# Folded input weights for a Fourier mixer, made in the FFN before it and kept in device memory

## The chip, the cores and the metric

One core of one Trainium2 chip. The time is the device time of one execution of the whole kernel in microseconds (us), as the median of several runs; less is better. The engines are TensorE (PE, matrix products, with its weight loads as PEld), VectorE (DVE), ScalarE (ACT), GpSimd (POOL) and SyncE (SP), whose queue issues nearly all transfers (DMA).

## The reference

One inference step of a small transformer-like trunk: 512 latent and 128 context tokens of width 1024, two layers. A layer is a half-step FFN, a token mixer, and another half-step FFN. Each sub-layer is wrapped in two RMS norms and is shifted, scaled and gated by vectors ("modulation") that come from a conditioning vector. Layer 0 mixes by a Fourier transform, layer 1 by attention.

```python
def _modulation(cond, w_mod, b_mod):
    m = jax.nn.silu(cond) @ w_mod + b_mod
    return m.reshape(cond.shape[0], N_MOD, D_MODEL)

def _half_ffn(x, m, k, g_pre, g_post, w1, w2):
    h = _modulated_prenorm(x, g_pre, m, k)
    return x + 0.5 * m[:, 3 * k + 2, None] * _rmsnorm(_swiglu(h, w1, w2), g_post)

def _fourier_mix(h, w_in, w_out):
    b, s, _ = h.shape
    u = (h @ w_in).reshape(b, s, N_FOURIER_GROUPS, FOURIER_GROUP_DIM)
    f = jnp.fft.fft2(u.astype(jnp.float32), axes=(1, 3), norm="ortho").real
    return f.astype(h.dtype).reshape(b, s, D_MODEL) @ w_out
```

The Fourier transform runs over the positions of a sequence and over the 128 channels of each of 8 groups. Context and latent tokens are separate sequences.

## The kernel before, in words

Six sub-layers follow one another: n = 0 is the first FFN (to about 440 us), n = 1 the Fourier mixer (to about 595), n = 2 and 3 are FFNs, n = 4 the attention, n = 5 the last FFN. Tokens lie in five tiles of 128: tiles 0 and 1, 3 and 4 are latent, 2 is the context tile.

**Products and splits.** Every fp32 operand is split into a high and a low half of a faster matmul type, and a product is three matmuls: high by high, low by high, high by low (`mm3`, lines 274 to 276). A split is a copy on ACT that gives the high half (line 260) and a subtraction on DVE that gives the low half (line 261). Weights come as *units* of 128 x 1024 numbers (512 KB). `unit(i)` makes sure that units up to i + 3 are sent: `send` loads one into a tile of the pool `raw` (4 buffers, through SP), prepares it by its kind, and splits it. The kind "fold" takes sum and difference of two halves of the weight on DVE before the split (lines 237 and 238); "block" splits into a ring of larger buffers; "plain" only splits.

**FFN.** The first layer runs in 22 blocks f of hidden channels (`w1_fast`), each with a fast scheme of seven products in place of eight. For it DVE adds gate and up weights (lines 228 to 230, tile `sums`, and 243), and these are split as well. A block first multiplies the gate's halves ("score" banks x, then y with the sums), then "turn" and "sum" banks follow. The second layer (`w2`) runs in five slices, after blocks 4, 8, 12, 16 and 22 (`SLICES`), tile by tile. While a slice of the second layer runs, the next block's gate and up units wait in two of the four raw buffers.

**Background work.** The modulation vectors of later sub-layers are matrix-vector products that PE doesn't do: `gemv` loads 512 KB of `w_mod_t` and multiplies and sums it twice on DVE (line 478, tile `junk`). These jobs are in a list, and `behind(n)` takes the next n of them. In FFN n, `BEHIND[n]` jobs are spread over the second layer's first four slices: 36 in the first FFN, 9 a slice. Others are taken at fixed places of the mixer.

**The end of the first FFN.** A finished tile goes through `chain` (its boundary): ACT squares it and sums (line 626), DVE multiplies by the gate vector (627, 630), POOL takes the power for the norm (610), DVE adds to the residual (633), and later it is transposed by PE, scaled and split into the mixer's input. The next tile's banks are first filled with partial sums by ACT (`seed`, line 913), and this waits until the tile that held the bank has gone through line 633.

**The mixer** (`fourier`). `pair_in` and the lines between multiply tokens with the eight four_in units into banks for even and odd channels; `sums` and `diffs` transform over positions, `channels` over channels; `pair_out` and what follows multiply with the eight four_out units. PSUM has 4 banks "main", 2 "score", 1 "turn" and 1 "sum"; a bank is free again when the split of its content is done.

**Order.** A scheduler orders each engine's instructions by estimated times and by priority; `high()` puts work ahead. An engine runs its own list in order, and waits at an instruction whose operands aren't there, with all behind it.

## Time and profile before

| | |
|---|---|
| median of 3 runs | 2216.58 us (2215.81 to 2218.85) |
| the profiled execution | 2218.44 us, its span 2216.7 us |
| mean clock granted to PE | 0.988 |
| busy: PE, DVE, ACT | 2173.2, 1743.1, 1179.2 us |
| transfers | 293.25 MB |

A line of the profile gives the line of the code, the engine, what is written from what, how many (x) and how long, and often the idle time just before and what ended it (`<-`). In the windows each engine's busy time in a stretch stands before its count, and the clock is a share of full speed.

### The profile page before, as it was taken

The numbers are of one execution on the slowest core, as the hardware profiler recorded it, in microseconds if no ns is written. First come the engines' busy times: TensorE is split into PE (matmuls) and PEld (weight loads), VectorE is DVE, ScalarE is ACT, GpSimd is POOL, SyncE is SP. The second block draws the span as 40 slices with busy tenths as digits, with TensorE's granted clock in tenths as the row PEclk, the third lists the DMA queues.
The fourth block names the chain that finished last, engine by engine and source line by source line (L and its number), as shares of the span: only waits on it lengthen the run. The fifth ranks groups of instructions, "written<-read, shape, count | busy, mean of one in ns | idle before, by whom it ended". The sixth has DMA issues, their size and how long they took to land.

```text
span 2216.7 us, 34573 instructions
## 1 busy us (share of the span) xinstructions
PE 2173.2 (98%) x13299; PEld 1997.3 (90%) x13299; DVE 1743.1 (79%) x3218; ACT 1179.2 (53%) x2221; POOL 45.3 (2%) x95
## 2 busy tenths in 40 slices
PE   7999999999899999999999999999999999999998
PEld 5999999977699999898998999989998899999997
DVE  5988898889798889878998898686556686766684
ACT  4544545464654545446544454466778654455452
POOL 0000000010100000001000000010000000000000
PEclk9999999998999999999999999999999999999999
DMA  8244344625324434452344444533333323322242
GB/s 315 86 143 162 134 152 139 216 86 178 116 96 138 159 132 147 148 196 99 109 147 146 141 143 146 179 99 101 111 101 110 119 81 105 115 95 77 95 129 100
DMA packets 85861, 293.25 MB, mean 132 GB/s; under 512 B 9696, under 2 KB 14656, under 8 KB 85568
## 3 DMA queue, kind: packets, MB, share of 16 engines
q1 hardware_dynamic: 85152, 290.39, 39.1%
q8 instruction: 104, 1.70, 0.3%
q10 hardware_dynamic: 544, 0.66, 0.1%
q14 instruction: 61, 0.50, 0.1%
HBM read 275.49 MB, written 11.58 MB: 130 GB/s over the span
## 4 chain that ended last, share of the span: by engine, by line
PE 89%; DVE 5%; ACT 3%; DMA 2%; issue 1%; POOL 0%; SPq 0%; DVEq 0%; POOLq 0%; ACTq 0%
PE main L275 12%; PE main L276 12%; PE main L274 12%; PE score L275 7%; PE score L276 7%; PE score L274 7%; PE turn L275 4%; PE turn L274 4%; PE sum L274 4%; PE sum L275 4%; PE turn L276 4%; PE sum L276 4%; DVE junk L478 1%; DMA raw<-in_w_mod_t 1%; PE sum L1569 1%
## 5 line engine op out<-in xcount | busy, mean ns | idle before, releaser
L260 ACT ACTIVATE hi<-raw 128x1024 fp32r<-128x1024 f32 (+1 forms) x388 | 371.1, 969 | 287.3 <-PE score L275 93.1
L261 DVE TENSOR_TENSOR lo<-raw,hi 128x1024 fp32r<-128x1024 f32 (+1 forms) x388 | 429.7, 1112 | 99.1 <-ACT hi L260 97.7
L274 PE MATMUL main<-hi,ring 128*128 128x512 f32 (+4 forms) x1089 | 412.3, 380 | 5.9 <-ACT hi L260 2.3
L275 PE MATMUL main<-lo,ring 128*128 128x512 f32 (+4 forms) x1089 | 410.8, 378 | 4.8 <-DVE lo L261 4.8
L276 PE MATMUL main<-hi,ring 128*128 128x512 f32 (+5 forms) x1089 | 410.3, 377 | 0.0
L478 DVE SCALAR_TENSOR_TENSOR junk<-raw,wide 128x1024 bf16<-128x1024 f32 x256 | 313.1, 1223 | 79.6 <-DMA raw<-in_w_mod_t 75.5
L276 PE MATMUL score<-ring,lo 128*128 128x320 f32 x916 | 283.4, 309 | 0.6 <-DVE lo L261 0.6
L275 PE MATMUL score<-ring,hi 128*128 128x320 f32 x916 | 283.7, 310 | 0.0
L274 PE MATMUL score<-ring,hi 128*128 128x320 f32 x916 | 283.3, 309 | 0.0
L274 PEld LDWEIGHTS main<-hi,ring 128*128 128x128 f32 (+2 forms) x1089 | 204.9, 189 | 47.9 <-ACT hi L260 3.6
L275 PEld LDWEIGHTS main<-lo,ring 128*128 128x128 f32 (+2 forms) x1089 | 205.9, 189 | 43.9 <-DVE lo L261 6.3
L276 PEld LDWEIGHTS main<-hi,ring 128*128 128x128 f32 (+2 forms) x1089 | 206.0, 189 | 40.5 <-issue 1.2
L274 PE MATMUL turn<-ring,hi 128*128 128x320 f32 x672 | 207.6, 309 | 3.0 <-ACT ring L260 2.9
L275 PE MATMUL turn<-ring,hi 128*128 128x320 f32 x672 | 208.3, 310 | 0.0
L274 PE MATMUL sum<-ring,hi 128*128 128x320 f32 x672 | 208.0, 310 | 0.1
L275 PE MATMUL sum<-ring,hi 128*128 128x320 f32 x672 | 207.8, 309 | 0.0
L276 PE MATMUL sum<-ring,lo 128*128 128x320 f32 x672 | 207.5, 309 | 0.0
L276 PE MATMUL turn<-ring,lo 128*128 128x320 f32 x672 | 207.0, 308 | 0.0
L942 ACT ACTIVATE y<-main 128x512 f32<-128x512 f32 x160 | 94.2, 591 | 208.2 <-PE main L276 207.0
L274 PEld LDWEIGHTS score<-ring,hi 128*128 128x128 f32 x916 | 172.4, 188 | 1.1
L276 PEld LDWEIGHTS score<-ring,lo 128*128 128x128 f32 x916 | 172.2, 188 | 1.0 <-DVE lo L261 1.0
L275 PEld LDWEIGHTS score<-ring,hi 128*128 128x128 f32 x916 | 172.3, 188 | 0.7
(318 smaller groups left out, 4138.8 us busy)
## 6 DMA issues: line engine op xcount, KB each, us to landing
raw<-in_w SPq DMA_DIRECT2D x272, 512.0 KB, 3.7
raw<-in_w_mod_t SPq DMA_DIRECT2D x128, 512.0 KB, 3.5
raw<-in_qkv SPq DMA_DIRECT2D x26, 512.0 KB, 3.5
spill<-ring SPq DMA_DIRECT2D x12, 640.0 KB, 3.3
ring<-spill SPq DMA_DIRECT2D x12, 640.0 KB, 7.4
raw<-in_bias SPq DMA_DIRECT2D x16, 448.0 KB, 3.7
first<-in_w_mod_k SPq DMA_DIRECT2D x8, 512.0 KB, 8.2
ring<-in_w_mod_k SPq DMA_DIRECT2D x8, 512.0 KB, 10.2
```

The costliest lines, as they stand in the source:

```text
L260: a = self.nc.scalar.activation(hi, src, AF.Copy)
L261: self.last_split = a, self.nc.vector.tensor_tensor(lo, src, hi.bitcast(F32), op=ALU.subtract)
L274: mm(out, whi, xhi, start=start, stop=False)
L275: mm(out, whi, xlo, start=False, stop=False)
L276: self.latest = mm(out, wlo, xhi, start=False, stop=stop)
L478: last = self.nc.vector.scalar_tensor_tensor(out=self.junk, in0=raw, scalar=1.0, in1=self.wide[:, cond, :], op0=ALU.mult, op1=ALU.mult, ac ...
L942: nc.scalar.activation(place(i, a), ps[a], AF.Copy)
L1569: mm = nc.tensor.matmul(out, cache_v[:, ds] if k is None else v[c // 2][c % 2][:, slot, ds], probs, start=n == 0, stop=n == len(tiles) - 1)
```

## The change

Eight jobs `fold_in` join the background list. Each loads one four_in unit, folds it on DVE, and stores it to device memory; the mixer then loads the folded units as plain ones. `BEHIND[0]` goes from 36 to 44, so that each of four slices takes two folds and nine modulation sums. Three modulation sums that the mixer's middle took are taken by blocks 19 to 21. Four splits of the mixer's middle are put at high priority. The odd bank of the first pair comes from "score" in place of "main". The second pair's output first asks for the units up to at + 7, that is all of four_out. The context tile is kept reversed in its 64 positions, so that 8 splits of a column fall away; constant tables follow.

```diff
-BEHIND = (36, 0, 36, 36, 0, 8)
+BEHIND = (44, 0, 36, 36, 0, 8)
...
+    def fold(self, a, b):
+
+        self.nc.vector.tensor_tensor(b, a, b, op=ALU.subtract)
+        self.nc.vector.scalar_tensor_tensor(out=a, in0=a, scalar=2.0, in1=b, op0=ALU.mult, op1=ALU.subtract)
+
+    def fold_in(self, k):
+
+        raw = self.raw_tile(self.io["four_in"][k])
+        a, b = (t.rearrange("p (m c) -> p m c", m=4) for t in (raw[:, :512], raw[:, 520:]))
+        self.fold(a[:, :, 2:], b)
+        self.nc.sync.dma_start(out=self.folded[k], in_=raw)
...
-                y = self.staged[:, 2 * j : 2 * j + n_pieces][:, :: -1 if j == CTX_TILE else 1]
+                y = self.staged[:, 2 * j : 2 * j + n_pieces]
+                if j == CTX_TILE:
+                    y = y[:, ::-1, :, ::-1]
...
-                if i in (1, 2):
-                    v, t, col = (2, SPECIAL, TOK + 1) if i == 1 else (5, 0, TOK)
+                if i == 1:
                     for c in range(0, NCH, 2):
-                        hi, lo = (h.block(part, c, 0)[:, :, col] for part in range(2))
-                        self.split(hi, lo, self.staged[:, v, c : c + 2, t])
+                        hi, lo = (h.block(part, c, 0)[:, :, TOK] for part in range(2))
+                        self.split(hi, lo, self.staged[:, 2, c : c + 2, SPECIAL])
...
                 w1_fast(a, half)
+                if n == 0 and a >= NF - 3:
+                    self.behind()
...
-                    self.units += [("foldblock" if k >= NWU else "fold", io["four_in"][k]) for k in range(NCH)]
+                    self.folded = [self.dram.tile([P, UNIT], F32, tag=f"fold{k}", name=self.name("fold")) for k in range(NCH)]
+                    self.units += [("block" if k >= NWU else "plain", self.folded[k]) for k in range(NCH)]
...
-            es, o = [self.bank() for _ in range(2)], self.bank()
+            es, o = [self.bank() for _ in range(2)], self.bank("main" if p else "score")
...
             p = [self.temp("left", F32R)[:, :322] for _ in range(2)]
-            self.split(*p, ps)
+            with high():
+                self.split(*p, ps)
...
-            self.split(*even_at(m, 0, 322), ps)
+            with high():
+                self.split(*even_at(m, 0, 322), ps)
...
-            self.behind((2, 2, 1, 0)[m])
+            self.behind(m < 2)
             self.unit(at + 3 + m)
...
+        self.unit(at + 4)
         pair_out(1)
...
+        for k in range(NCH):
+            self.background.insert(4 + 11 * k // 2, partial(self.fold_in, k))
```

What it does to the order shows at three places. First DVE's list at the end of the second slice (about 213 to 219 us of the profile before). `junk` is a modulation sum, `left` and `right` are the running block's intermediate products, `lo` of a `raw` is the next gate's low half, and `sums` the first of the three operations that add gate and up. Before:

```order
L478 SCALAR_TENSOR_TENSOR junk,mod<-raw_1969,wide 128x1024
L871 TENSOR_TENSOR left_1995<-score_852,left_1992 128x320
L478 SCALAR_TENSOR_TENSOR junk,mod<-raw_1969,wide 128x1024
L875 TENSOR_TENSOR left_2027<-left_1995,turn_1974 128x320
L261 TENSOR_TENSOR lo_1999<-raw_1996,hi_1998 128x1024
L879 TENSOR_TENSOR left_2027<-left_2027,sum_2030 128x320
L228 TENSOR_TENSOR sums_2033<-raw_1996,raw_2031 128x512
```

And in the changed kernel, where `raw_1992` is the slice's second fold:

```order
L888 TENSOR_TENSOR left_2055<-left_2055,sum_2058 128x320
L251 TENSOR_TENSOR raw_1992<-raw_1992 128x504
L486 SCALAR_TENSOR_TENSOR junk,mod<-raw_1997,wide 128x1024
L252 SCALAR_TENSOR_TENSOR raw_1992<-raw_1992 128x4x126
L486 SCALAR_TENSOR_TENSOR junk,mod<-raw_1997,wide 128x1024
L895 TENSOR_TENSOR right_2056<-left_2023,turn_2002 128x320
L269 TENSOR_TENSOR lo_2027<-raw_2024,hi_2026 128x1024
L900 SCALAR_TENSOR_TENSOR left_2023<-sum_2058,left_2023 128x320
L896 TENSOR_TENSOR right_2056<-right_2056,right_2021 128x320
L228 TENSOR_TENSOR sums_2061<-raw_2024,raw_2059 128x512
```

The fold's two operations stand around the last sum, and the gate's low half and the sums stand behind three more of the running block's products. SP's list of the same slice has the transfers, here in the changed kernel (before, it held the nine loads of `w_mod_t` and then the two of the next block, `in_w`):

```order
L203 DMA raw_1883<-in_w_mod_t 128x1024
L203 DMA raw_1915<-in_four_in 128x1024
L203 DMA raw_1920<-in_w_mod_t 128x1024
L259 DMA fold_80<-raw_1915 128x1024
L203 DMA raw_1952<-in_w_mod_t 128x1024
L203 DMA raw_1956<-in_w_mod_t 128x1024
L203 DMA raw_1988<-in_w_mod_t 128x1024
L203 DMA raw_1992<-in_four_in 128x1024
L203 DMA raw_1997<-in_w_mod_t 128x1024
L203 DMA raw_2024<-in_w 128x1024
L203 DMA raw_2059<-in_w 128x1024
L259 DMA fold_81<-raw_1992 128x1024
```

Two loads and two stores are added, and the load after the first store takes the buffer that this store reads. Second, DVE in the last slice of the first FFN (about 447 to 451 us before): `main_1047` and `main_1048` are the two halves of tile 1, `main_1049` the first half of the context tile, `col` the norm's column. Before:

```order
L609 SCALAR_TENSOR_TENSOR col_4279<-col_4275 128x1
L630 TENSOR_TENSOR main_1048<-main_1048,total_3829 128x512
L633 SCALAR_TENSOR_TENSOR ring_4102<-main_1047,col_4279,ring_4102 128x512
L633 SCALAR_TENSOR_TENSOR ring_4102<-main_1048,col_4279,ring_4102 128x512
L627 TENSOR_TENSOR main_1049<-main_1049,square_3832 128x512
```

In the changed kernel tile 1 is `main_1055` and `main_1056`, the context tile `main_1057`:

```order
L635 TENSOR_TENSOR main_1057<-main_1057,square_3884 128x512
L617 SCALAR_TENSOR_TENSOR col_4322<-col_4316 128x1
L617 SCALAR_TENSOR_TENSOR col_4333<-col_4329 128x1
L638 TENSOR_TENSOR main_1056<-main_1056,total_3881 128x512
L641 SCALAR_TENSOR_TENSOR ring_4162<-main_1055,col_4333,ring_4162 128x512
L641 SCALAR_TENSOR_TENSOR ring_4162<-main_1056,col_4333,ring_4162 128x512
```

The context tile's gate product has moved from behind tile 1's four operations to ahead of them. Third, DVE in the mixer's middle (about 519 to 524 us before): `rms` is the split of the small middle sums, `left` and `total` are the splits of sums and differences over positions, `raw` with line 237 or 251 a fold of four_out. Before:

```order
L237 TENSOR_TENSOR raw_4920<-raw_4920 128x512
L1142 TENSOR_TENSOR ring_4930<-raw_4928,ring_4930 8x1024
L238 SCALAR_TENSOR_TENSOR raw_4920<-raw_4920 128x512
L261 TENSOR_TENSOR rms_4934<-main_4935,rms_4933 8x322
L261 TENSOR_TENSOR left_4966<-main_4955,left_4965 128x322
```

And in the changed kernel:

```order
L269 TENSOR_TENSOR left_5002<-main_4991,left_5001 128x322
L269 TENSOR_TENSOR total_5014<-main_5005,square_5013 126x384
L269 TENSOR_TENSOR left_5028<-main_5017,left_5027 128x322
L251 TENSOR_TENSOR raw_4956<-raw_4956 128x512
L1154 TENSOR_TENSOR ring_4966<-raw_4964,ring_4966 8x1024
L269 TENSOR_TENSOR total_5040<-main_5031,square_5039 126x384
L252 SCALAR_TENSOR_TENSOR raw_4956<-raw_4956 128x512
L269 TENSOR_TENSOR rms_4970<-main_4971,rms_4969 8x322
```

Three of the splits now stand ahead of the third fold, and the middle's split has gone behind it.

More of the change, by code (lines that the diff above doesn't have):

```diff
@@ L233, in send @@
             raw = self.raw_tile(src)
-            a, b = raw[:, one], raw[:, two]
-            if "rows" not in kind:
-                a, b = a.rearrange("p (m c) -> p m c", m=4)[:, :, 2:], raw[:, 520:].rearrange("p (m c) -> p m c", m=4)
-            nc.vector.tensor_tensor(b, a, b, op=ALU.subtract)
-            nc.vector.scalar_tensor_tensor(out=a, in0=a, scalar=2.0, in1=b, op0=ALU.mult, op1=ALU.subtract)
+            self.fold(raw[:, one], raw[:, two])
         elif kind == "up":
@@ L245, in send @@
         n = at.stop - at.start
-        if kind in ("block", "foldblock", "foldrowsblock"):
+        if kind in ("block", "foldblock"):
             hi, lo = (self.ring(F32R)[:, :n] for _ in range(2))
@@ L1053, in list_units @@
                 if i == 0:
-                    self.units += [("foldblock" if k >= NWU else "fold", io["four_in"][k]) for k in range(NCH)]
+                    self.folded = [self.dram.tile([P, UNIT], F32, tag=f"fold{k}", name=self.name("fold")) for k in range(NCH)]
+                    self.units += [("block" if k >= NWU else "plain", self.folded[k]) for k in range(NCH)]
                     self.units += [("plain", io["dft"][k]) for k in range(3)]
-                    self.units += [("foldrowsblock" if u in (3, 4) else "foldrows", io["four_out"][u]) for u in range(NCH)]
+                    self.units += [("foldblock" if u in (3, 4) else "fold", io["four_out"][u]) for u in range(NCH)]
                 else:
@@ L1126, in fourier @@
         for k in range(NCH):
-            even_in(k, token(k, LAT + 64, TOK + 2), even)
+            even_in(k, token(k, LAT + 63, TOK + 1), even)
         plain, ends = self.ring(F32)[:64, :504], self.ring(F32R)
@@ L1175, in positions @@
             p = [self.temp("left", F32R)[:, :322] for _ in range(2)]
-            self.split(*p, ps)
+            with high():
+                self.split(*p, ps)
             ps = diffs(m)
             q = [self.temp(kind, F32R)[:126, :384] for kind in ("square", "total")]
-            self.split(*q, ps)
+            with high():
+                self.split(*q, ps)
             return p, q
@@ L1188, in channels @@
                 mm(x5, mid_w[0][:, 256 + 72 * m : 328 + 72 * m], p[i], start=m == i == 0, stop=False)
-            self.split(*even_at(m, 0, 322), ps)
+            with high():
+                self.split(*even_at(m, 0, 322), ps)
             ps = self.bank("score")[:, :384]
             self.mm3(ps, mid_w[0][:126, P : 2 * P], mid_w[1][:126, P : 2 * P], *q, True, True)
-            self.split(*odd_at(m, 0, 384), ps)
+            with high():
+                self.split(*odd_at(m, 0, 384), ps)
         ready = positions(0)
@@ L1707, in host_inputs @@
     ctx = np.arange(64)
+    back = ctx[::-1]
     big = np.zeros((3, P, UNIT))
@@ L1711, in host_inputs @@
     big[0, :, :516] = sums.reshape(2, P, 258).transpose(1, 0, 2).reshape(P, 516)
-    big[0, :65, 516:581] = wave(np.cos, np.arange(65), np.arange(65), CTX) / 128
+    big[0, :65, 516:581] = wave(np.cos, np.r_[64, back], np.arange(65), CTX) / 128
     big[0, 65, 581:838] = wave(np.cos, [256], np.r_[256, near], LAT) / 512
@@ L1726, in host_inputs @@
     small = np.zeros((P, 208))
-    small[:64, :64] = -wave(np.sin, ctx, ctx, CTX) / 128
+    small[:64, :64] = -wave(np.sin, back, ctx, CTX) / 128
     small[:64, 64:128] = -small[:64, :64]
```

## The prediction

> **What bounds the kernel now.** I read the page first: the span and the share of TensorE.
>
> ```profile
> span 2216.7 us, 34573 instructions
> ...
> PE 2173.2 (98%) x13299; PEld 1997.3 (90%) x13299; DVE 1743.1 (79%) x3218; ACT 1179.2 (53%) x2221; POOL 45.3 (2%) x95
> ```
>
> TensorE (PE) is idle for 2216.7 − 2173.2 = 43.5 us in all. So only three things count: whether an edit ends a wait of PE, starts one, or changes the clock that PE is granted. Next, busy time by stretches of the span: the end of a second-layer slice of the first FFN (200 to 240), the last blocks of that FFN (400 to 436), and the middle of the Fourier mixer (520 to 560). Columns are PE, PE's weight loads, DVE, ACT and POOL, then the granted clock, the DMA share and GB/s.
>
> ```profile
> 200.00:220.00 20.00, 20.00 (x114) 18.20 (x114) 18.60 (x33) 8.69 (x14) 0.00 (x0) 1.00 0.57 184
> 220.00:240.00 20.00, 20.00 (x139) 20.00 (x138) 19.80 (x34) 10.59 (x18) 0.00 (x0) 1.00 0.32 106
> 400.00:436.00 36.00, 36.00 (x221) 33.85 (x220) 29.53 (x49) 14.79 (x24) 0.00 (x0) 1.00 0.73 257
> 520.00:540.00 20.00, 16.37 (x78) 13.18 (x76) 19.21 (x33) 7.27 (x13) 0.00 (x0) 0.83 0.59 197
> 540.00:560.00 20.00, 17.65 (x51) 12.48 (x49) 16.59 (x32) 7.07 (x13) 0.00 (x0) 0.66 0.57 185
> ```
>
> In the FFN PE never stops and DVE runs just below it (38.40 of 40 us from 200 to 240). In the mixer DVE is as full, PE waits, and the clock drops. The timeline of PE there has these waits (start, length, instruction, and in brackets the idle time before it and what ended it):
>
> ```profile
> 451.00 0.50 PE L274 MATMUL main<-hi,ring 128*128 128x512 f32 x1 [0.56 <-ACT main L913]
> 473.91 0.49 PE L274 MATMUL main<-hi,ring 128*128 128x504 f32 x1 [1.24 <-DVE ring L633]
> 483.05 0.58 PE L275 MATMUL main<-lo,ring 128*128 128x256 f32 x1 [3.37 <-DVE lo L261]
> 522.10 0.39 PE L274 MATMUL main<-hi,ring 128*126 128x256 f32 x1 [1.77 <-DVE rms L261]
> 539.49 0.41 PE L274 MATMUL score<-left,hi 128*128 128x322 f32 x1 [1.85 <-DVE ring L261]
> 560.00 0.73 PE L274 MATMUL main<-hi,ring 128*128 128x512 f32 x2 [2.35 <-ACT hi L260]
> ```
>
> And the windows cut at the edges of the slow clock:
>
> ```profile
> 475.00:482.00 7.00, 4.68 (x25) 3.19 (x23) 6.56 (x16) 3.13 (x11) 0.59 (x1) 1.00 0.25 75
> 482.30:489.10 6.80, 6.05 (x19) 4.38 (x20) 6.80 (x10) 2.21 (x3) 0.00 (x0) 0.50 0.36 109
> 523.30:530.10 6.80, 6.80 (x26) 5.75 (x24) 6.80 (x13) 0.93 (x2) 0.00 (x0) 0.50 0.55 180
> 540.30:554.00 13.70, 13.70 (x35) 9.66 (x36) 12.10 (x26) 4.18 (x7) 0.00 (x0) 0.50 0.58 180
> 560.80:564.10 3.30, 2.84 (x7) 2.08 (x8) 0.41 (x1) 0.30 (x1) 0.00 (x0) 0.51 0.46 159
> ```
>
> The waits of 3.37, 1.77, 1.85 and 2.35 us are each followed by a stretch at clock 0.50; the one of 1.24 is not (clock 1.00 from 475 to 482). A usual stretch is 6.8 us long and costs half of that, 3.4 us. So a wait of about 1.8 us or more costs its own length and, most times, 3.4 us again.
>
> **The change, part by part.** Prices first, by shape, then transfers (KB, us from issue to landing):
>
> ```profile
> L478 DVE SCALAR_TENSOR_TENSOR junk<-raw,wide 128x1024 bf16<-128x1024 f32 x256 | 313.1, 1223 | 79.6 <-DMA raw<-in_w_mod_t 75.5
> L260 ACT ACTIVATE hi<-sums 128x1024 fp32r<-128x1024 f32 x79 | 83.9, 1062 | 121.3 <-DVE sums L230 109.4 <-PE sum L275 9.8 <-DVE right L887 1.1
> L237 DVE TENSOR_TENSOR raw<-raw 128x504 f32<-128x504 f32 x8 | 5.3, 680 | 2.1 <-DMA raw<-in_four_in 2.1
> L238 DVE SCALAR_TENSOR_TENSOR raw<-raw 128x504 f32<-128x504 f32 x8 | 5.3, 680 | 0.1
> ```
>
> ```profile
> raw<-in_w_mod_t SPq DMA_DIRECT2D x128, 512.0 KB, 3.5
> spill<-ring SPq DMA_DIRECT2D x12, 640.0 KB, 3.3
> raw<-in_four_in SPq DMA_DIRECT2D x8, 512.0 KB, 3.8
> x_out<-ring SPq DMA_DIRECT2D x8, 256.0 KB, 2.1
> ```
>
> **Folds in the FFN's slices.** Two fold jobs join the nine modulation sums of each of four slices. A fold is 0.68 + 0.68 = 1.36 us of DVE; with its load and store it holds a raw buffer for 3.8 + 1.4 + 3.3 = 8.5 us, where a sum holds one for 3.5 + 2 × 1.22 = 5.9. The store of 512 KB is in no row: it lies between those of 256 KB (2.1) and 640 KB (3.3), and I take 3.3, the nearer in size. This is DVE at the end of the slice that closes at 221 us, then PE there:
>
> ```profile
> 194.95 1.23 DVE L478 SCALAR_TENSOR_TENSOR junk<-raw,wide 128x1024 bf16<-128x1024 f32 x1
> 197.18 1.23 DVE L478 SCALAR_TENSOR_TENSOR junk<-raw,wide 128x1024 bf16<-128x1024 f32 x1 [0.99 <-DMA raw<-in_w_mod_t]
> 203.37 1.23 DVE L478 SCALAR_TENSOR_TENSOR junk<-raw,wide 128x1024 bf16<-128x1024 f32 x1 [1.12 <-DMA raw<-in_w_mod_t]
> 215.79 1.22 DVE L261 TENSOR_TENSOR lo<-raw,hi 128x1024 fp32r<-128x1024 f32 x1
> 218.77 0.69 DVE L230 TENSOR_TENSOR sums<-raw,raw 128x512 f32<-128x512 f32 x1
> 220.59 1.23 DVE L261 TENSOR_TENSOR lo<-sums,hi 128x1024 fp32r<-128x1024 f32 x1
> ```
>
> ```profile
> 221.47 0.31 PE L274 MATMUL score<-ring,hi 128*128 128x320 f32 x1
> 223.37 0.31 PE L275 MATMUL score<-ring,hi 128*128 128x320 f32 x1
> ```
>
> Only two of the four raw buffers turn over there; gate and up of the running block hold the others. So sums wait on loads (0.99, 1.12). The third sum ends at 194.95 + 1.23 = 196.2. In its buffer the first fold's weights land at 200.0, are folded by 201.4, and are stored by 204.7; only then can the sixth sum's load go out, and it lands at 208.2 instead of 203.3. From the sixth sum on DVE has no rest. Before, it took 215.79 − 203.37 = 12.4 us from there to the low half of the next gate. Now 1.9 us of splits fall into the pause ahead of it, and the second fold (1.36) and a small operation of 0.4 come in: about 12.3 us, so the low half starts near 220.5 instead of 215.8. The three operations for the sums of gate and up end, before, at 218.77 + 0.69 = 219.5, that is 3.7 us after that point. Now about 1.6 us of short products stand between as well: 220.5 + 3.7 + 1.6 = 225.8, and up to 1 us later where the low half itself lies in the queue longer. ACT's high half takes 1.06 more: 227.
>
> PE comes at 221.47. Its pace is (223.37 − 221.47)/13 = 0.146 us a matmul. Before, 12 matmuls use the gate and then the sums are wanted at 223.2. In the new order both halves of the gate come first, 24 matmuls, until 225.0. Six more need the high halves alone. So PE waits from 225.0 to between 227 and 228, and some tenths more for low halves: I take 2.6 us a slice, with ends of 0 (the store lands in 2.1, and the pauses swallow the fold) and 3.8. Four slices: 10.4 us, ends 0 and 15. A wait of that size gets the half clock in about 7 of 10 cases (four of four rows from 1.77 up, but here PE may wait in two pieces): 4 × 0.7 × 3.4 = 9.5. Sum **+19.9**, ends 0 and 29.
>
> The Trainium skill (TensorE: Matmul & The Clock Gate, Part 1 and "HAM oscillation") states that the clock halves after an idle window of some 3.4 us that runs freely, and that gaps over that length are to be avoided. By that rule these gaps of 2.6 us would cost 10.4 and not 19.9. The trace differs: half clock followed 1.77 us.
>
> **Three sums behind blocks 19 to 21.** 3 × 2 × 1.22 = 7.3 us more for DVE in some 36 us, where it has 36.00 − 29.53 = 6.5 to spare. PE was never stopped there, so the operands are ready ahead of it, and that lead hides the 0.8 left over: 0, with ends of 0 and +2 (a lead that is gone; nothing here can gain, since PE is full).
>
> **The last slice's context tile.** DVE and ACT before, as the third token tile's start is prepared:
>
> ```profile
> 447.45 0.22 DVE L609 SCALAR_TENSOR_TENSOR col<-col 128x1 f32<-128x1 f32 x2
> 448.78 1.41 DVE L633 SCALAR_TENSOR_TENSOR ring<-main,col,ring 128x512 f32<-128x512 f32 x2 [0.49 <-POOL col L610]
> 450.49 0.70 DVE L627 TENSOR_TENSOR main<-main,square 128x512 f32<-128x512 f32 x1 [0.30 <-ACT y L626]
> ```
>
> ```profile
> 449.77 0.60 ACT L626 ACTIVATE y<-main 128x512 f32<-128x512 f32 x1 [0.59 <-PE main L276]
> 450.35 0.59 ACT L913 ACTIVATE main<-y 128x512 f32<-128x512 f32 x1
> ```
>
> PE's next tile waits for ACT to fill the bank (L913), that for L633, that for POOL's power of the column. In the new order the context tile's gate product stands ahead of tile 1's column and L633. It can't start before 450.49, since ACT's square waits for PE. After it 0.7 + 0.2 + the way over POOL (447.67 to 448.78, 1.1): L633 at 452.4 instead of 448.78, its first half done at 453.1, the bank filled at 453.75. PE starts at 453.8 instead of 451.00: **+2.8**, ends 0 and 4, and 3.4 for the clock in 3 of 4 cases, **+2.6**.
>
> **The mixer.** Taking the odd bank of the first pair from the other pool ends the wait of 1.24: **−1.2**; after it nothing shorter waits. The wait of 3.37 stays: DVE between 462 and 483 does the boundary's chain, which the change leaves as it is but for 0.4 us of tiny splits; the 10.9 us of folds that leave the mixer (16 × 0.68) lay before and behind it, under a busy PE. The three waits after 520 (1.77 + 1.85 + 2.35 = 6.0) all end with a split that stood behind folds and sums on DVE, or with weights folded too late. There DVE is busy 19.21 of 20 us. Three sums fewer (7.3 us), splits at the front, and all output weights requested before the second pair: I take 0.85 × 6.0 = **−5.1**. The clock lost in their stretches is (6.8 + 13.7 + 3.3)/2 = 11.9; three quarters of it, **−8.9**. Ends: 0, and all of it, −17.9.
>
> Sum: 19.9 + 2.8 + 2.6 − 1.2 − 5.1 − 8.9 = +10.1. On the profiled execution's own 2218.4 (span 2216.7 and 1.7 around it) that is 2228.5. That execution lies 1.9 above the median of 2216.6, so on the median's footing the forecast is **2226.6**. By the page's rule for the four slices alone, the sum would be 0.6.
>
> **The rivals.**
>
> *The slices take the folds for nothing* (26%). For it: DVE has pauses of 0.99 and 1.12 us and more in front, and PE's order was moved to ask for the sums 1.8 us later. Against it: from the sixth sum on there is no pause left. It decides at 225.0: if the high half of the sums is there, no slice waits. Then 2216.6 + 2.8 − 1.2 − 17.9 + 1 (a rest at the slices) = 2201.3, faster.
>
> *Only a window idle as a whole halves the clock* (17%). A PE that is back after 2.6 us keeps full speed, and so does the one at 453.8. The mixer's gain stays, since its stretches are there: 10.4 + 2.8 − 1.2 − 5.1 − 8.9 = −2.0, giving 2214.6, the same as before. Against it: 1.77 us was enough at 522. The Trainium skill's rule (TensorE: Matmul & The Clock Gate, Part 1) is this rival's.
>
> *The mixer's waits don't yield* (15%). The chain from the product through ACT and DVE to the next bank is what is late, not the queue, and four_out's loads are late as well. Then the gain is −1.2 − 2 and the sum 19.9 + 5.4 − 3.2 = 22.1: 2238.7.
>
> **How the numbers follow.** The forecast has 42%, and its own range is 2217 to 2236 (two thirds of the slices' ends either way). Faster and slower both have weight, so the range reaches to the first rival's centre and the last one's: 2201 to 2239, which leaves out half of each, 13 + 7%. A measurement here can tell about 0.2%, 4.4 us. Faster by more: 24 of the first rival, 4 of the second: 0.28. Within: 2 of the first, 9 of the second, 6 of the forecast: 0.17. Slower: 36 of the forecast, 4 of the second, 15 of the last: 0.55.
>
> **What would show it.** In the changed profile: PE waits near 145, 225, 300 and 378 us, each released by ACT's or DVE's halves of the sums, with the clock at 0.50 behind; a wait of some 3 us before the tile that starts at 451; none at 474, 522 and 539. If those windows show PE 20.00 of 20.00, the first term fails and the kernel is faster. If the waits are there at clock 1.00, the second rival is right.

## The result, and the profile after

| | before | after |
|---|---|---|
| median of 4 runs each | 2217.02 us (2215.81 to 2218.85) | 2243.11 us (2240.06 to 2248.72) |
| ratio after : before, 95% interval | | 1.012 (1.0095 to 1.0144) |
| the profiled execution, its span | 2218.44, 2216.7 | 2240.06, 2238.3 |
| mean clock granted to PE | 0.988 | 0.985 |

The changed kernel is slower by 26 us, where 10 were forecast: the sign was right, the size was not, and the time lies above the range. The profiled execution is the fastest of its four (the others reach 2248.72 at a clock of 0.982), so the trace accounts for 21.6 us. The head of its page:

```profile
span 2238.3 us, 34596 instructions
...
PE 2179.4 (97%) x13299; PEld 2000.4 (89%) x13299; DVE 1742.4 (78%) x3214; ACT 1175.8 (53%) x2217; POOL 44.5 (2%) x95
```

DVE and ACT have four instructions fewer each: four splits of a column have fallen away, not eight. PE has 58.9 us of idle time instead of 43.5. To see where, I cut the span at three marks that both kernels have. The first is PE's product of `coef` with the identity near the end of the first FFN (400.31 before, 427.80 after). The second is the start of the tile behind the context tile (451.00, 483.01). The third is the first product behind the mixer (596.15, 618.48). Busy times by these stretches (columns as in the prediction), before:

```profile
220.00:300.00 80.00, 80.00 (x478) 74.64 (x477) 71.00 (x118) 41.30 (x64) 0.00 (x0) 1.00 0.42 139
...
400.30:451.00 50.70, 50.13 (x281) 44.91 (x278) 41.90 (x75) 21.27 (x46) 1.61 (x3) 1.00 0.61 216
451.00:596.10 145.10, 130.04 (x625) 101.00 (x625) 123.00 (x217) 85.35 (x174) 9.23 (x14) 0.89 0.35 116
596.10:2216.00 1619.90, 1608.20 (x10040) 1496.54 (x10040) 1240.73 (x2364) 875.24 (x1694) 32.02 (x70) 1.00 0.38 124
```

and after:

```profile
140.00:220.00 80.00, 77.91 (x447) 71.71 (x446) 66.02 (x108) 37.81 (x60) 0.00 (x0) 0.98 0.45 152
220.00:300.00 80.00, 75.27 (x415) 68.70 (x414) 66.44 (x109) 35.00 (x55) 0.00 (x0) 0.94 0.43 145
300.00:380.00 80.00, 76.80 (x452) 70.58 (x451) 67.19 (x112) 37.62 (x60) 0.00 (x0) 1.00 0.46 158
380.00:427.80 47.80, 43.58 (x263) 41.75 (x262) 42.63 (x75) 17.55 (x29) 0.00 (x0) 0.89 0.44 143
427.80:483.00 55.20, 50.32 (x280) 44.85 (x277) 46.92 (x84) 23.39 (x51) 1.61 (x3) 1.00 0.66 231
483.00:618.40 135.40, 123.79 (x625) 97.27 (x625) 109.71 (x190) 83.19 (x166) 8.32 (x14) 0.93 0.36 117
618.40:2238.00 1619.60, 1607.56 (x10040) 1495.83 (x10040) 1240.63 (x2364) 875.28 (x1694) 32.11 (x70) 1.00 0.38 124
```

By the marks, the FFN up to the first lost 427.80 − 400.31 = 27.5 us, the stretch to the next tile 55.2 − 50.7 = 4.5, the mixer gained 145.2 − 135.5 = 9.7, and the rest gained 0.7: 21.6. In the four FFN rows PE is idle for 2.1 + 4.7 + 3.2 + 4.2 = 14.2 us. The clock takes 80 × 0.02 + 80 × 0.06 + 47.8 × 0.11 = 11.7 more. Before, neither was there.

PE's timeline of the changed kernel has these waits:

```profile
147.18 0.41 PE L282 MATMUL score<-ring,hi 128*128 128x320 f32 x1 [0.53 <-ACT left L876]
...
150.69 0.42 PE L282 MATMUL score<-ring,hi 128*128 128x320 f32 x1 [1.47 <-ACT hi L268]
...
229.82 0.41 PE L284 MATMUL score<-ring,lo 128*128 128x320 f32 x1 [2.56 <-DVE lo L269]
...
232.45 0.63 PE L282 MATMUL score<-ring,hi 128*128 128x320 f32 x1 [0.53 <-ACT left L876]
...
237.49 0.64 PE L282 MATMUL score<-ring,hi 128*128 128x320 f32 x1 [1.47 <-ACT hi L268]
...
314.46 0.42 PE L284 MATMUL score<-ring,lo 128*128 128x320 f32 x1 [1.11 <-DVE lo L269]
...
397.28 0.41 PE L284 MATMUL score<-ring,lo 128*128 128x320 f32 x1 [2.15 <-DVE lo L269]
...
441.55 0.28 PE L595 MATMUL turn<-ident,coef 128*16 128x128 f32 x1 [1.17 <-DVE right L895]
...
483.01 0.50 PE L282 MATMUL main<-hi,ring 128*128 128x512 f32 x1 [3.72 <-ACT main L922]
...
515.89 0.39 PE L283 MATMUL main<-lo,ring 128*128 128x256 f32 x1 [3.17 <-DVE lo L269]
...
561.43 0.50 PE L282 MATMUL main<-hi,ring 128*128 128x512 f32 x1 [3.89 <-ACT ring L268]
```

Three of the four slices have three waits, not one: for the gate's low half, then 0.53 and 1.47. The first slice has only the pair. The pair comes with the same lengths in all four: PE puts both halves of the gate's products into the same bank, one after the other, so it waits 0.53 until ACT has copied the first (L876), and then 1.47 for the sums' high half. The windows around some of them:

```profile
146.40:160.00 13.60, 11.51 (x64) 10.71 (x63) 11.22 (x18) 5.36 (x9) 0.00 (x0) 0.87 0.36 114
229.00:240.00 11.00, 8.18 (x31) 7.38 (x32) 7.89 (x13) 5.46 (x9) 0.00 (x0) 0.59 0.20 61
310.00:325.00 15.00, 11.80 (x75) 10.74 (x75) 13.61 (x22) 6.85 (x11) 0.00 (x0) 1.00 0.46 146
560.00:580.00 20.00, 18.34 (x56) 13.29 (x57) 14.07 (x26) 8.42 (x15) 0.00 (x0) 0.66 0.48 151
```

The slow clock follows 2.56 us and 3.89 us, and in the first slice (0.87) it follows the pair alone, where no wait is longer than 1.47. The waits from 314 on (1.11, 0.53, 1.47) leave it at 1.00.

**Inside the slice** that closes at 237, DVE after:

```profile
210.78 1.23 DVE L486 SCALAR_TENSOR_TENSOR junk<-raw,wide 128x1024 bf16<-128x1024 f32 x1 [2.08 <-DMA raw<-in_w_mod_t]
...
215.57 1.22 DVE L486 SCALAR_TENSOR_TENSOR junk<-raw,wide 128x1024 bf16<-128x1024 f32 x1 [0.55 <-DMA raw<-in_w_mod_t]
...
224.67 0.67 DVE L251 TENSOR_TENSOR raw<-raw 128x504 f32<-128x504 f32 x1
...
227.01 1.21 DVE L486 SCALAR_TENSOR_TENSOR junk<-raw,wide 128x1024 bf16<-128x1024 f32 x1
...
228.55 1.21 DVE L269 TENSOR_TENSOR lo<-raw,hi 128x1024 fp32r<-128x1024 f32 x1
...
233.19 0.68 DVE L230 TENSOR_TENSOR sums<-raw,raw 128x512 f32<-128x512 f32 x1
```

and SP, which issues the transfers:

```profile
208.72 0.33 SPq L259 DMA_DIRECT2D fold<-raw  x1
212.03 2.74 SPq L203 DMA_DIRECT2D raw<-in_w_mod_t  x3
```

The first store holds its buffer until a load can go out at 212.03, 3.3 us after it. The modulation sums behind it still pause for loads (0.55 at 215.57, 0.47 at 218.54), for four loads go out between 212.03 and 215.05, and they land after 3.4, 5.1, 5.5 and 6.2 us; from there on DVE works without a pause. The second fold starts at 224.67 and the last modulation sum ends at 228.2, in the middle of the next block. Only then comes the gate's low half, for which PE waits until 229.82. The sums of gate and up end at 233.9. Yet their high half on ACT waits longer still:

```profile
236.05 0.44 ACT L892 ACTIVATE right<-score 128x320 f32<-128x320 f32 x1 [3.30 <-PE score L284]
236.39 1.05 ACT L268 ACTIVATE hi<-sums 128x1024 fp32r<-128x1024 f32 x1
```

In the changed order ACT first copies the bank that PE has just filled with the second half of the next gate's products (L892), and the sums' high half, which PE wants next, stands behind that copy. So PE waits for the way through both, 0.44 + 1.05 less the overlap, which is the 1.47, although DVE was done some 2 us earlier. (In the fourth slice it was the same 2.2; in the first and third these sums ended 0.1 and 0.5 us before PE wanted the high half, so there DVE's lateness is in the wait as well.) Before, the high half stood only behind the copy of the running block: that one began at 218.17, the high half at 219.50, well ahead of PE's need at 223.2.

**In the mixer** the wait of 3.89 is new. ACT, and then DVE, ahead of it:

```profile
559.99 1.06 ACT L268 ACTIVATE ring<-raw 128x1024 fp32r<-128x1024 f32 x1 [5.47 <-DVE raw L252]
560.95 0.80 ACT L268 ACTIVATE ring<-score 128x322 fp32r<-128x322 f32 x2
```

```profile
557.52 0.69 DVE L251 TENSOR_TENSOR raw<-raw 128x512 f32<-128x512 f32 x1
558.13 1.22 DVE L486 SCALAR_TENSOR_TENSOR junk<-raw,wide 128x1024 bf16<-128x1024 f32 x1
559.27 0.69 DVE L252 SCALAR_TENSOR_TENSOR raw<-raw 128x512 f32<-128x512 f32 x1
```

PE wants the split of `score` (the second ACT row). It stands on ACT behind the high half of a four_out unit, which waits 5.47 us for DVE to fold that unit, and the fold stands behind and between modulation sums.

### The profile page after: what moved, and what is told of

It reads as the page before. It is cut to its first block, busy times and chain, and to the rows that moved or that the text cites. A ratio compares the mean times of both kernels' runs of the same rounds, so it can differ in the third digit from the quotient of the medians.

```text
span 2238.3 us, 34596 instructions
## 1 busy us (share of the span) xinstructions
PE 2179.4 (97%) x13299; PEld 2000.4 (89%) x13299; DVE 1742.4 (78%) x3214; ACT 1175.8 (53%) x2217; POOL 44.5 (2%) x95
## 4 chain that ended last, share of the span: by engine, by line
PE 81%; DVE 8%; DMA 6%; ACT 3%; issue 2%; POOL 0%; SPq 0%; DVEq 0%; POOLq 0%; ACTq 0%
PE main L282 11%; PE main L283 11%; PE main L284 11%; PE score L282 7%; PE score L284 7%; PE score L283 7%; PE sum L282 4%; PE turn L283 4%; PE sum L283 4%; PE turn L282 4%; PE turn L284 4%; PE sum L284 4%; DMA raw<-in_w_mod_t 3%; DVE junk L486 3%; DVE lo L269 2%
## 5 line engine op out<-in xcount | busy, mean ns | idle before, releaser
L282 PE MATMUL main<-hi,ring 128*128 128x512 f32 (+4 forms) x1083 | 409.2, 379 | 7.6 <-ACT ring L268 3.9
L283 PE MATMUL main<-lo,ring 128*128 128x512 f32 (+4 forms) x1083 | 406.2, 375 | 4.8 <-DVE lo L269 4.6
L284 PE MATMUL main<-hi,ring 128*128 128x512 f32 (+4 forms) x1083 | 405.6, 375 | 0.0
L282 PE MATMUL score<-ring,hi 128*128 128x320 f32 x916 | 287.0, 313 | 8.1 <-ACT hi L268 5.9
L283 PE MATMUL score<-ring,hi 128*128 128x320 f32 x916 | 286.2, 312 | 0.0
L282 PEld LDWEIGHTS main<-hi,ring 128*128 128x128 f32 (+2 forms) x1083 | 203.1, 188 | 48.4 <-ACT ring L268 4.4
L283 PEld LDWEIGHTS main<-lo,ring 128*128 128x128 f32 (+1 forms) x1083 | 203.4, 188 | 43.9 <-DVE lo L269 5.9
L284 PEld LDWEIGHTS main<-hi,ring 128*128 128x128 f32 (+1 forms) x1083 | 203.0, 187 | 40.6 <-issue 0.4
L282 PEld LDWEIGHTS score<-ring,hi 128*128 128x128 f32 x916 | 174.6, 191 | 12.0 <-ACT hi L268 7.2
L283 PEld LDWEIGHTS score<-ring,hi 128*128 128x128 f32 x916 | 174.7, 191 | 0.7
```

Source lines behind the costliest of these rows:

```text
L282: mm(out, whi, xhi, start=start, stop=False)
L283: mm(out, whi, xlo, start=False, stop=False)
L284: self.latest = mm(out, wlo, xhi, start=False, stop=stop)
```

## The experiments

All twelve by the same marks, against before's profile (us; the ratio with its 95% interval is of the medians, against runs of before on the same chip). The three columns of times are from one profiled execution each, with the clock that it got; e3, e4 and e7 were run twice, the others four times or more:

| run | FFN to mark 1 | to mark 2 | mixer | ratio |
|---|---|---|---|---|
| after | +27.5 | +4.5 | −9.7 | 1.012 (1.0095 to 1.0144) |
| e1_no_folds | +0.1 | +3.2 | −7.9 | 0.9993 (0.9983 to 1.0002) |
| e2_middle_high | +1.8 | +2.1 | −3.7 | 1.0004 (0.9994 to 1.0013) |
| e3_folds_only | +19.3 | −0.4 | −4.1 | 1.007 (1.005 to 1.0091) |
| e4_no_store | +12.4 | +7.8 | −6.4 | 1.0066 (1.0045 to 1.0086) |
| e5_sums_early | +5.9 | +0.7 | −12.8 | 0.9982 (0.9972 to 0.9992) |
| e6_send_after | +0.3 | +2.1 | −3.7 | 0.9997 (0.9988 to 1.0005) |
| e7_no_fold_dve | +16.7 | +5.9 | −8.8 | 1.0058 (1.004 to 1.0077) |
| e8_both | +5.6 | +0.9 | −8.3 | 1.0003 (0.9994 to 1.0013) |
| e9_nine_jobs | +4.7 | +10.6 | −8.9 | 1.0043 (1.0027 to 1.006) |
| e10_sums_spread | +13.6 | +1.9 | −6.1 | 1.0052 (1.0032 to 1.0072) |
| e11_middle_sums | +1.5 | +0.6 | +3.6 | 1.0036 (1.0025 to 1.0047) |
| e12_late_blocks | +2.2 | +1.0 | −13.6 | 0.9948 (0.9934 to 0.9961) |

### e1_no_folds: the folds go back to the mixer

```diff
-BEHIND = (44, 0, 36, 36, 0, 8)
+BEHIND = (36, 0, 36, 36, 0, 8)
...
-                    self.units += [("block" if k >= NWU else "plain", self.folded[k]) for k in range(NCH)]
+                    self.units += [("foldinblock" if k >= NWU else "foldin", io["four_in"][k]) for k in range(NCH)]
...
-        for k in range(NCH):
-            self.background.insert(4 + 11 * k // 2, partial(self.fold_in, k))
```

> The changed kernel with only the eight fold jobs taken back: the first FFN's slices hold nine modulation sums each, as before, and the mixer folds four_in itself. Theory A (the fold jobs make DVE late at the slice ends): the waits near 147, 230, 315 and 400 us and their slow clock go, some 28 us, and the tile that waited 3.7 us at 483 as well; 2211 to 2216 us. Theory B (the loss comes from the other edits, the three sums behind blocks 19 to 21 or the new priorities): 2235 or more.

The kind `foldin` folds a four_in unit as `fold` did before. Median 2214.75 against 2217.53, the same within what can be told. The slices' waits are gone, and mark 1 is where it was before: the fold jobs cost 27 us in the changed kernel's profiled execution, its slow clock included. The tile's wait, which the expectation had going with them, is still 2.68 us. The mixer's new wait is there without the folds, longer still, and so is most of the gain:

```profile
534.84 0.79 PE L286 MATMUL main<-hi,ring 128*128 128x512 f32 x1 [5.22 <-ACT ring L272]
```

```profile
454.20:591.50 137.30, 123.89 (x625) 96.67 (x625) 117.71 (x205) 84.69 (x169) 9.23 (x14) 0.93 0.36 115
```

The mixer takes 137.3 us with the folds in it and 135.5 without. By this pair their leaving is worth some 2 us; by e3, which moves the folds and nothing else, 4.1.

### e2_middle_high: e1 with the middle's split at high priority

```diff
-        self.split(*middle, sums(4))
+        ps = sums(4)
+        with high():
+            self.split(*middle, ps)
```

> As e1_no_folds, and the split of the small middle sums (rms) put at high priority too. Theory: the changed kernel's wait of 3.89 us at 561 comes from this split, which now stands behind the four splits that went to high priority, so the first score product closes late and its split on ACT stands behind a fold; with it in front that wait goes: 4 us and up to 7 us of slow clock less than e1_no_folds. Rival (the wait is due to the weights' fold and split on ACT and DVE alone): within 2 us of e1_no_folds and a wait of 3 us or more in the mixer's middle.

The wait stays, 4.67 us at 534.78. So the middle's split was not what held ACT up; this theory fell. The median is 3.6 us above e1's, and a wait of 1.69 for a weight's high half stands at 559.98.

### e3_folds_only: the kernel before with the fold jobs alone

The new functions and the folded units in device memory are as in the change.

```diff
-BEHIND = (36, 0, 36, 36, 0, 8)
+BEHIND = (44, 0, 36, 36, 0, 8)
...
+        for k in range(NCH):
+            self.background.insert(4 + 11 * k // 2, partial(self.fold_in, k))
```

> The kernel before with only the eight fold jobs (nine sums and two folds a slice, folded units loaded by the mixer). Theory A: the slice ends wait as in the changed kernel, 25 to 30 us lost before 450 us, and the mixer gains little: 2240 to 2248. Theory B: 2217 within 5.

The slices show the same waits, so they come from the fold jobs and from nothing else in the change. The second slice:

```profile
227.60 0.63 PE L288 MATMUL score<-ring,lo 128*128 128x320 f32 x1 [2.48 <-DVE lo L273]
231.16 0.41 PE L286 MATMUL score<-ring,hi 128*128 128x320 f32 x1 [0.53 <-ACT left L879]
234.67 0.42 PE L286 MATMUL score<-ring,hi 128*128 128x320 f32 x1 [1.47 <-ACT hi L272]
```

But the clock falls little behind them, and not at all in the other three slices, of which the third is shown:

```profile
227.00:239.00 12.00, 9.31 (x49) 8.37 (x50) 9.42 (x15) 5.46 (x9) 0.00 (x0) 0.86 0.29 91
310.00:325.00 15.00, 12.06 (x76) 11.25 (x77) 13.54 (x22) 6.43 (x11) 0.00 (x0) 1.00 0.34 112
```

Of the 19.3 us up to mark 1, 13.6 are idle time by the windows and some 2 the clock; the rest I can't place. That is less than the 25 to 30 us expected, and the median of 2232.67 lies below the 2240 to 2248. A wait here has a sure part, its length, and a part that falls or doesn't. Mark 2 is not late in this run, so the late tile is not the folds' doing.

### e4_no_store and e7_no_fold_dve: which part of the job costs?

e4 has no stores, and the mixer loads four_in as it is. e7 keeps load and store, without the two DVE operations.

```diff
         self.fold(a[:, :, 2:], b)
-        self.nc.sync.dma_start(out=self.folded[k], in_=raw)
...
-                    self.units += [("block" if k >= NWU else "plain", self.folded[k]) for k in range(NCH)]
+                    self.units += [("block" if k >= NWU else "plain", io["four_in"][k]) for k in range(NCH)]
```

```diff
         raw = self.raw_tile(self.io["four_in"][k])
-        a, b = (t.rearrange("p (m c) -> p m c", m=4) for t in (raw[:, :512], raw[:, 520:]))
-        self.fold(a[:, :, 2:], b)
         self.nc.sync.dma_start(out=self.folded[k], in_=raw)
```

> The changed kernel without the stores of the folded units; the fold jobs still load and fold, and the mixer loads four_in unfolded, so this part of the product is left out. Theory C (the store keeps the raw buffer, so that the sixth sum's load goes out 3.3 us late): the waits at the slice ends fall to half or less, 12 to 20 us less than the changed kernel. Rival D (the folds' 2.7 us of DVE a slice are what is late, the buffers are not): within 5 us of the changed kernel.

> The changed kernel whose fold jobs load and store but don't fold (DVE's 2.7 us a slice are left out, so the product isn't the reference's). PE's order at the slice ends stays the changed one. Theory F (0.53 + 1.47 us a slice belong to the new order of PE and ACT, and only the wait for the gate's low half belongs to DVE's lateness): the pairs of 0.5 and 1.5 us stay in all four slices, the waits for the low half (2.56, 1.11, 2.15) fall below 1 us; 2225 to 2234. Rival (all of it is lateness): all waits at the slice ends fall alike; 2218 to 2224.

e4 still has 10.0 us of waits in the slices (1.44 + 1.26 + 0.41 in the third), e7 10.9 (0.70 + 0.53 + 1.47 in the third). In e7 the pair of 0.53 and 1.47 stays in three slices of four, and no other wait there is longer than 0.96. In e4 the waits fall on neighbouring places of the order and come to as much. By these waits neither the store nor the DVE work carries most of the cost, where the expectation for e4 had half of them going with the store. By mark 1 e4 saves more, 15.1 of 27.5, but 11.7 of the 27.5 were slow clock, which neither kernel drew in the slices, and e4 had a faster clock ahead of them as well (0.99 to 140 us, 0.96 in the changed kernel). What both kernels keep is eleven jobs a slice.

### e9_nine_jobs: two folds in nine jobs

```diff
-BEHIND = (44, 0, 36, 36, 0, 8)
+BEHIND = (36, 0, 36, 36, 0, 8)
...
-                if n == 0 and a >= NF - 3:
+                if n == 0 and a in (6, 7, 10, 11, 14, 15, 17, 18, 19, 20, 21):
...
-            self.background.insert(4 + 11 * k // 2, partial(self.fold_in, k))
+            self.background.insert(11 * (k // 2) + (3, 7)[k % 2], partial(self.fold_in, k))
```

> The changed kernel with all its folds, but nine background jobs a slice as before (two folds and seven sums); the eight displaced sums are taken by blocks 6, 7, 10, 11, 14, 15, 17 and 18. Theory G (the slices are paced by two raw buffers at about 3 us a job, so that the tenth and eleventh job fall into the next block; their kind matters little): the waits at the slice ends go, with PE's order as before, and short waits of up to 1 us for DVE appear in the blocks; the first FFN loses 3 to 10 us instead of 29, and the whole is 2217 to 2227. Rival (a fold is what hurts, by its store and its place): waits of 1 us and more stay at the slice ends, 2232 or more.

All folds and stores are done, in nine jobs a slice, and the displaced sums go behind blocks. The slices' waits are gone but for tenths (0.41, 0.65, 0.45 and 0.45 up to mark 1), and with them the slow clock: +4.7 in place of +27.5, of which the windows show 2.1 as idle. So two jobs fewer end the waits, though all folds and stores are there. Their number isn't told apart from the time for which jobs hold the two raw buffers. By the prediction's prices (5.9 us a sum, 8.5 a fold with its store, 5.2 without the store, 7.1 without the DVE work) a slice's jobs hold each of the two buffers for an estimated 26.6 us before, 29.2 in e9, 31.8 in e4, 33.7 in e7 and 35.1 in the changed kernel. (This is a rough measure: at the end of a slice four loads are under way at once, as seen above.) The waits come in the same order: 0, 2.1, 10.0, 10.9 and 14.2. DVE's own work doesn't order them: it is 22.0 us a slice both before and in e7. The price shows up behind the slices, where the last blocks' sums stand on DVE ahead of the boundary:

```profile
466.36 0.80 PE L282 MATMUL main<-hi,ring 128*128 128x512 f32 x1 [8.53 <-ACT main L922]
```

### e10_sums_spread and e11_middle_sums: where else can the sums go?

Both are e9 with other blocks (the folds' places in e10's list follow); e11 also gives the mixer's middle its sums back.

```diff
-                if n == 0 and a >= NF - 3:
+                if n == 0 and a in (5, 6, 7, 9, 10, 11, 13, 14, 15, 17, 18):
```

```diff
-                if n == 0 and a >= NF - 3:
+                if n == 0 and a in (6, 7, 10, 11, 14, 15, 17, 18):
...
-            self.behind(m < 2)
+            self.behind((2, 2, 1, 0)[m])
```

> The changed kernel with all its folds and nine or ten jobs a slice, the eleven other sums in blocks 5, 6, 7, 9, 10, 11, 13, 14, 15, 17 and 18, none in blocks 19 to 21. Theory H (the wait of the tile after the context tile, 8.53 us in e9_nine_jobs and 3.72 in the changed kernel, comes from sums that blocks 19 to 21 leave in DVE's queue): it falls to 1 us or less, and with theory G the kernel loses 3 to 8 us before 450 us and has the mixer's gain: 2212 to 2220. Rival (the folds or the reversed context tile cause it): the wait stays above 2.5 us, 2222 or more.

> As e10_sums_spread, but only the eight displaced sums in blocks (6, 7, 10, 11, 14, 15, 17 and 18), and the mixer's middle takes its five sums as before the change. Theory H: the tile's wait is 1 us or less here too. If the three sums less in the middle are what ended the old waits at 522 and 539, they or others come back: 4 to 8 us more in the mixer than in e10_sums_spread; if the splits at high priority did it, the mixer is within 3 us.

With none behind blocks 19 to 21 the tile's wait falls from 8.53 to 1.36 (e10, where 1 or less was expected) and 0.16 (e11). Eleven sums behind earlier blocks cost 13.6 us there (e10), with waits of 0.5 to 1.9 us from 224 on, so room behind blocks is limited too, and e10's 2228.25 lies above the 2212 to 2220 expected; eight cost 1.5 (e11). And with five sums in the middle again, the mixer gains nothing:

```profile
453.10:601.80 148.70, 131.46 (x625) 99.94 (x625) 116.53 (x202) 84.50 (x170) 8.26 (x14) 0.88 0.34 114
```

e11 has the four high splits, the other bank and the folds outside. Yet its mixer takes 148.7 us and before's 145.2. So what the change won there needs the three sums out of the middle. Whether that alone would win it, without the splits' priority and the other bank, no run shows.

### e5, e6, e8 and e12: e1 with the middle relieved

e5 takes the last two sums out of the mixer's middle (five are taken by blocks), e6 asks for the next output unit behind `channels`, e8 does both, e12 is e5 with later blocks. The first cut is e5's and the second e6's, each on top of e1; the third is e12's against e5.

```diff
-                if n == 0 and a >= NF - 3:
+                if n == 0 and a in (7, 11, 15, 18, 19):
...
-            self.behind(m < 2)
```

```diff
-            self.unit(at + 3 + m)
             channels(m, *ready)
+            self.unit(at + 3 + m)
```

```diff
-                if n == 0 and a in (7, 11, 15, 18, 19):
+                if n == 0 and a in (15, 16, 17, 18, 19):
```

> As e1_no_folds, and no modulation sums in the mixer's middle: all five are taken by blocks 7, 11, 15, 18 and 19 of the first FFN. Theory E (the wait of 5.22 us at 534.8 in e1_no_folds is ACT's: the high half of a block weight stands ahead of the score's split, and waits for a fold that stands behind two sums, 4.9 us, on DVE): that wait shrinks to under 1 us, and with its slow clock the kernel gains 5 to 9 us on e1_no_folds, 2206 to 2210. Rival (the weight's transfer or the position splits are late anyway): a wait of 3 us or more stays there, 2213 to 2218. In DVE's order tile 1's L645 stands ahead of the context tile again, so the wait of 2.68 us at 454 should be 1 us or less.

> As e1_no_folds, with the call that sends the next output weight moved behind the channels' products (the two lines swapped), so that in ACT's order the two splits of the first score products stand ahead of the block weight's high half; the two sums stay on DVE. Theory E: the wait of 5.22 us at 534.8 shrinks to under 2 us (DVE's own part of the split may still stand behind a sum), and weights sent later make waits of up to 3 us near 555; 2208 to 2214. Rival: the wait stays at 4 us or more.

> e5_sums_early and e6_send_after together. Theory E: the middle of the mixer has no wait over 1 us; 2203 to 2209. Rival: within 2 us of e5_sums_early, or slower by waits for output weights near 555.

> As e5_sums_early, with the five sums in blocks 15 to 19 instead of 7, 11, 15, 18 and 19. In e5_sums_early the first FFN lost 6 us to waits for DVE at the slice ends, behind the sums in blocks 7, 11 and 15. Theory: only one such place is left, so 3 to 5 us of them come back, and the tile's wait stays under 1 us, since blocks 20 and 21 stay free: 2208 to 2212. Rival (the place of the sums doesn't matter, five sums more in the FFN cost 5 us wherever they are): within 2 us of e5_sums_early.

In e5 the 5.22 of e1 shrinks to 2.81 (under 1 was expected), and the mixer is 12.8 us shorter than before, but the FFN pays 5.9. In e6 the wait is gone, which shows that the unit's high half on ACT was in the way. But units then come late, and six waits of 0.5 to 2.4 us between 541 and 560 take its place. e8 has 0.53 there and 0.89, 0.80 and 1.68 later: the two edits don't add up. All three medians (2213.96, 2217.37, 2217.83) lie above what was expected of them. e12, in which the five sums stand behind blocks 15 to 19, has 2.44 us in the middle:

```profile
532.33 0.50 PE L286 MATMUL main<-hi,ring 128*128 128x512 f32 x1 [2.44 <-ACT ring L272]
```

```profile
454.20:585.80 131.60, 120.63 (x625) 93.66 (x625) 113.58 (x198) 85.29 (x170) 9.29 (x14) 0.97 0.34 112
```

Its median is 2206.53 against 2218.18 for before on the same chip. It beats both kernels, and by the ratios to before (0.9948 and 1.012, on different chips) the changed one by 1.7%, more than 30 us. It is the change without the folds in the FFN, with no sums in the mixer's middle. That is better than the 2208 to 2212 expected: the FFN pays 2.2 where e5 paid 5.9.

## Why the prediction was right or wrong

**The slices' folds: the step that failed.** The term was 19.9 us, one wait of 2.6 a slice for the sums' high half and the half clock behind it in 7 of 10 cases. Measured were 27.5: 14.2 of idle time and 11.7 of clock by the windows, and 1.6 that these don't show. The mechanism was a DVE that falls behind because folds hold raw buffers longer, and this held: 208.72 to 212.03 is the 3.3 taken for a store. Two things in the step were wrong.

First, the gate's low half. The forecast put it at 220.5, 11.4 us after PE's last product with w2 (209.15 before), and charged some tenths for it. It started at 228.55, 14.5 us after that point (214.05). The load behind the first store landed at 215.5, not ahead of the end of w2 as forecast; the modulation sums after it paused twice more for loads, which took up to 6.2 us where the forecast had 3.5 to 3.8; and the second fold and the last modulation sum came in the middle of the next block. That made waits of 2.56, 1.11 and 2.15 in three slices, 5.8 in all.

Second, the sums' high half. The forecast had 2.6 a slice, from a DVE that is late; paid were 0.53 + 1.47 = 2.0, and only a part of it is DVE's: its sums of gate and up ended 0.1, 2.2, 0.5 and 2.2 us before PE wanted their high half, which takes ACT 1.06, and the copy that stands ahead on ACT made the wait 1.47 each time. (The 0.53, for the gate's own bank, had no place in the forecast.) The pair is paid in every slice of the changed kernel and of e3, and in none of e1's or e9's.

e4, e7 and e9 show that two jobs more a slice make most of the lateness even with their store or their DVE work left out; number of jobs and time in the buffers aren't told apart. That the scheduler chooses this order for eleven jobs and not for nine is what the runs show together; a kernel with ACT's order alone changed, or with a third buffer for the jobs, wasn't tried.

**The clock.** 9.5 were forecast for the slices and 11.7 measured, which is partly luck: with nearly the same idle time e3 drew some 2 and lost 19.3 up to mark 1. In the profiled run the slices with waits of 2.56 and 2.15 got the slow clock and that with 1.11 did not. The prediction's 1.8 us is no lower limit: the first slice's clock fell to 0.75 from 150 to 155 behind 0.53 and 1.47, and in e3 the same pair left it at 1.00. There, too, a wait of 2.48 was followed by 0.86 on average and one of 1.63 by none. The Trainium skill (TensorE: Matmul & The Clock Gate, Part 1) has the clock fall after a window of about 3.4 us that is idle; here half clock also came behind idle times of 1.47, 2.15 and 2.56 us, and the rival that went by that rule gave 2214.6 and fell. For e3's later slices the rule's answer, no loss, is what the trace has.

**Blocks 19 to 21.** Forecast 0, at most 2. They cost more, in two places: 1.17 us at 441.55, where one of these sums waited for its load with the product that PE needed behind it on DVE, and part of the tile's wait.

**The context tile.** 2.8 were forecast and 3.2 came (3.72 against 0.56), without the slow clock for which 2.6 were set down (the stretch to 483 is at 1.00). That the stretch came out near its forecast, +4.5 for 5.4, is luck: 1.17 at 441.55 came in and the clock's 2.6 did not. The cause was only half seen. The context tile's gate product does stand ahead of tile 1's column now, at 479.34 behind a pause of 0.47, about 1.1 us of delay. Sums have a part as well: in e9, e10 and e11 the product stands behind the column again, and the wait is 8.53 with sums behind blocks 19 to 21 and 1.36 and 0.16 without. With the change's three sums but no folds it is 2.68, 1.35 and 2.02 (e1, e2, e6), so how much of the 3.72 is whose stays open; no run separates the two parts.

**The mixer.** −15.2 were forecast and −9.7 came. The wait of 1.24 is gone, as said; with the old bank it is there (2.02 in e3). The 3.37 stays, at 3.17. The waits of 1.77, 1.85 and 2.35 are gone too, but the new one of 3.89, with the clock at 0.66 from 560 to 580, gives back 3.9 of the 1.2 + 5.1 us of idle time. By the windows PE's idle time fell from 15.1 to 11.6, 3.5 in place of 6.3, and what the clock took from 145.1 × 0.11 = 16.0 to 135.4 × 0.07 = 9.5, 6.5 in place of 8.9. The rival of a mixer that doesn't yield spoke of four_out units that come late, and that was the piece missing from the forecast: to ask for units earlier and to fold them on a DVE with sums in its list puts a late unit ahead of a ready split on ACT. e6 shows that it stood in the way, e5 and e12 that fewer sums shorten it. Of the reasons given for the gain, the sums that left the middle are the one it can't do without (e11): with all five back, the splits' priority, the other bank and the folds' leaving gave nothing together. The folds' leaving is worth 2 to 4 us (e1, e3).

**The sum.** FFN +27.5 for 19.9, the stretch behind it +4.5 for 5.4, the mixer −9.7 for −15.2, elsewhere −0.7: 21.6 in the profiled execution for 10.1. The medians differ by 4.5 more: the profiled execution lies 3.1 below the changed kernel's median, two of whose runs got clocks of 0.982 and 0.984, and before's lies 1.4 above its own. Two ends that the forecast had named, the slices' term at 29 and a mixer that gives 5.5 less, would together have made 2226.6 + 9.1 + 5.5 = 2241.2, beyond the range's 2239: they were never taken together, though both come from the same crowded DVE.

## What to carry to other kernels

Background jobs that share a few buffers are paced by how many there are and how long each holds a buffer, not by an engine's work in them alone: ask when the last one ends against the point at which its engine is next needed, and count every operation behind it on that engine. If a job moves out of one stage that has little room into another, look for a stage with room in both engine and buffers; here the cheapest place tried for the middle's sums was behind blocks of the FFN that are not the last ones. A fold, a split or a copy that may be late should not stand on an in-order engine ahead of one that is ready and that the bound engine waits for.

## What the runs showed of the hardware that was not expected

The same waits at the same places met different clocks. The four slices of the changed kernel and of e3 have idle times alike to 1 us (14.2 and 13.6 in all). The clock fell to 0.98, 0.94 and 0.89 in three of the former's four stretches, and in e3 only in the second, to 0.98. Even 0.53 and 1.47, alone in the first slice, were followed by the slow clock in one kernel and not in the other. The changed kernel's runs differ by 8.7 us (2240.06 to 2248.72, at clocks from 0.987 to 0.982), before's four by 3.0, but 27 runs of before on e5's chip by 10.1 (2211.96 to 2222.05, clocks from 0.995 to 0.987), so this isn't a matter of the slices alone. A forecast for one execution of such a kernel should hold a range of some 10 us for this.
